# Attention scores: the products of two heads alternate between the upper and lower 64 rows of TensorE

## The chip, the cores and the metric

The kernel runs on one core of one Trainium2 chip. The metric is the device time of one execution in microseconds (us). Times of single runs are given as the median of three; the profile and the trace come from one further execution. TensorE is the matrix engine (PE in the rows, its weight loads PEld), VectorE is DVE, ScalarE is ACT, GpSimd is POOL, SyncE (SP) issues most DMAs.

## What is computed

Two decoder layers on 256 tokens of width 2048. Each layer has four mixers of width 512 side by side (a gated one, differential attention, dilated attention, a convolution), an output projection, and a feed-forward part of width 8192. The change touches the scores of the two attention mixers. Both come down to the same form for a pair of heads with 64 channels each:

```
s = q . k / sqrt(64)                       (per head, causal, 256 queries, 256 keys)
s = s - slope * distance,  masked where the distance is negative
p = softmax(s)                              (dilated: three patterns, summed by multiplicity)
```

Differential attention takes the difference of the two heads' probabilities; dilated attention keeps the two heads apart. Each mixer has four such pairs of heads, so there are eight pairs in a layer and 16 in all.

## The kernel before

**Large matmuls.** The weights (some 380 MB) come as 738 units of 128 x 1024 fp32. Each is split into a high part (ScalarE, tile `h`) and a low part (VectorE, tile `l`) in fp32r, a form of fp32 that TensorE takes in one pass, and three products of high and low parts are summed in PSUM (tiles `acc`, `acct`, `accu`, `accg`). The stages of a layer follow each other: the input projection with the mixers woven in, the output projection, then four blocks of the feed-forward part. A sublayer ends with a normalisation that the next projection must wait for (`sublayer_end`, tile `xhl`).

**The order of work.** It is written out by a planner in the program, before anything runs. Every engine is wrapped by `Paced`, which adds an estimated price per instruction (for a matmul: columns / 2400 us, four times that when the weights are plain fp32, plus 0.003). The mixers are generators: a `yield engine, time` means that the next instructions are written once TensorE's estimated clock has come that far. Between the large matmuls `pump()` runs whatever is due: splits of weights, evacuations, and steps of the mixers. On the chip each engine then takes its instructions in that order and waits on semaphores.

**The scores.** `scores` (lines 772 to 798) serves one pair of heads and is called by `dil_gen` and `diff_gen`, 16 times in all. `q` and `k` hold the two heads' channels in 128 partitions: head 0 in partitions 0 to 63, head 1 in 64 to 127, with tokens along the columns; they are plain fp32. The tile `ps` (tag `sc`) has 2 x 512 columns of PSUM, one bank per head, of which 384 are used: 128 for the first block of queries against the first block of keys, 256 for the second block of queries against both blocks. `COL` (line 770) names these two column ranges. For each head an identity matmul (`identb` times `ndist_sb`, bf16, all 128 rows) writes the negative distances into the 384 columns, and two products of 64 rows add `q . k` on top. Then VectorE takes the maximum over both heads (lines 785 and 787), ScalarE the exponential, and `give("sc")` frees the tile. `take("sc")` at its head makes the call wait until the tile is free.

The profile gives nearly all instructions the line of the wrapper, L99, so groups are told apart by the tiles' names: `sc<-ndist_sb,identb` is the identity matmul, `sc<-qk` a product of queries and keys.

Of the kernel before, what the change touches and what calls it, by code (L numbers as in the profile page):

```python
# [19 lines left out]
P = 128  # L20
L = 2
D = 2048
T = 256
# [111 lines left out]
def trunk_kernel(ctx, tc, xT, xt, wu, par, gpost, gw, gb, lam, ndist, mult, out):  # L135
# [16 lines left out]
    G, PE = nc.gpsimd, Paced(nc.tensor, _pe_cost)  # L152
# [147 lines left out]
    def take(name):  # L300
        while name in locks:
            yield None, lambda: name not in locks
        locks.add(name)
        yield PE, freed.get(name, 0.0) + D_

    def give(name):
        locks.discard(name)
        freed[name] = max(V.t, S.t)
# [103 lines left out]
    def unit_c(rhs):  # L412

        force(lambda: held[0] < 4)
        ps = pacc.tile([P, 2 * T], F32, tag="acc", name=f"acc{unit[0]}")
        for half in range(2):
            u = unit[0]
            unit[0] += 1

            for part in "hl":  # L420
                use(u, part == "l")
                for k in range(HALF):
                    if k % 2 == 0:
                        pump()
                    mm_c(ps, u, k, rhs, half * HALF + k, parts=part)
            done(u)
        return ps
# [342 lines left out]
    COL = (slice(0, P), slice(P, 3 * P))  # L770

    def scores(pr, q, k, s2, nm):

        yield PE, V.t + D_
        yield from take("sc")
        ps = psc.tile([P, 2, GW], F32, tag="sc", name="sc")
        for j in range(2):
            r = slice(64 * j, 64 * j + 64)
            PE.matmul(ps[:, j, 0 : 3 * P], identb, ndist_sb, start=True, stop=False)
            PE.matmul(ps[:, j, 0:P], q[r, 0:P], k[r, 0:P], start=False, stop=False)  # L780
            PE.matmul(ps[:, j, P : 3 * P], q[r, P:T], k[r, 0:T], start=False, stop=True)
        scored.append(1)
        yield V, PE.t + D_
        m = tiny.tile([P, 2, 2], F32, tag=nm + "m", name="m", bufs=1)
        V.reduce_max(m[:, :, 0], ps[:, :, 0:P], axis=AX.X)
        yield V, 0.0
        V.reduce_max(m[:, :, 1], ps[:, :, P : 3 * P], axis=AX.X)
        yield V, V.t
        V.tensor_tensor(m, m, nsl[:, pr], ALU.mult)
        yield S, V.t + D_  # L790
        l = tiny.tile([P, 2, 2], F32, tag=nm + "l", name="l", bufs=1)
        for j in range(2):
            for b in range(2):
                S.activation(s2[:, j, COL[b]], ps[:, j, COL[b]], AF.Exp, bias=m[:, j, b : b + 1], scale=SLOPE_PAIRS[pr][j], accum_out=l[:, j, b : b + 1])
            yield S, 0.0
        give("sc")
        yield V, S.t + D_
        return l
# [32 lines left out]
    def dil_gen(lane, li, pr, q, k, v, mhl, ready):  # L831
        nm = f"n{lane}"
        p = mx.tile([P, 2, 3 * P], F32, tag=nm + "s2", name="p2", bufs=1)
        yield from scores(4 + pr, q, k, p, nm)
        l = tiny.tile([P, 2, 2], F32, tag=nm + "l2", name="l2", bufs=1)
        for j in range(2):
            for b in range(2):
                V.scalar_tensor_tensor(p[:, j, COL[b]], p[:, j, COL[b]], 1.0, mult_sb[:, COL[b]], ALU.mult, ALU.mult, accum_out=l[:, j, b : b + 1])
                yield V, 0.0
        V.reciprocal(l, l)  # L840
        yield PE, V.t + D_
        pt = yield from transposed(p[:, 0], nm)
        yield from take("o")
        o = po.tile([P, 2, P], F32, tag="o", name="od")
        values(o, slice(0, 64), pt, v, slice(128 * pr, 128 * pr + 64))
        pt = yield from transposed(p[:, 1], nm)
        values(o, slice(64, 128), pt, v, slice(128 * pr + 64, 128 * pr + 128))
        yield S, PE.t + D_
        on = mx.tile([P, 2, P], F32, tag=nm + "on", name="on", bufs=1)
        for b in range(2):  # L850
            for j in range(2):
                S.activation(on[:, b, 64 * j : 64 * j + 64], o[:, b, 64 * j : 64 * j + 64], AF.Copy, scale=l[:, j, b : b + 1])
        give("o")
        yield from turned(on, mhl, pr, 1.0, ready)

    def diff_gen(lane, li, h, q, k, v, mhl, ready):
        nm = f"n{lane}"
        p = mx.tile([P, 2, 3 * P], F32, tag=nm + "s2", name="p2", bufs=1)
        l = yield from scores(h, q, k, p, nm)
        V.reciprocal(l, l)  # L860
        yield V, V.t
        V.tensor_scalar(l[:, 1], l[:, 1], lamv[:, li : li + 1], None, ALU.mult)
        yield S, V.t + D_
        for b in range(2):
            S.activation(p[:, 1, COL[b]], p[:, 1, COL[b]], AF.Copy, scale=l[:, 1, b : b + 1])
        for b in range(2):
            yield V, S.t + D_ if b == 0 else 0.0
            V.scalar_tensor_tensor(p[:, 0, COL[b]], p[:, 0, COL[b]], l[:, 0, b : b + 1], p[:, 1, COL[b]], ALU.mult, ALU.subtract)
        yield PE, V.t + D_
        pt = yield from transposed(p[:, 0], nm)  # L870
        yield from take("o")
        o = po.tile([P, 2, P], F32, tag="o", name="ob")
        values(o, slice(0, P), pt, v, slice(h * P, (h + 1) * P))
        yield S, PE.t + D_
        ss = tiny.tile([P, 2], F32, tag=nm + "oss", name="oss", bufs=1)
        on = mx.tile([P, 2, P], F32, tag=nm + "on", name="onb", bufs=1)
        for b in range(2):
            S.activation(on[:, b, :], o[:, b, :], AF.Square, accum_out=ss[:, b : b + 1])
        yield V, S.t + D_
        rs = yield from rsqrt(ss, P, [P, 2], nm + "ors")  # L880
        yield S, V.t + D_
        for b in range(2):
            S.activation(on[:, b, :], o[:, b, :], AF.Copy, scale=rs[:, b : b + 1])
        give("o")
        yield from turned(on, mhl, 4 + h, subg[:, li : li + 1], ready)
# [62 lines left out]
    for li in range(L):  # L948
# [72 lines left out]
        for n, (kind, grp, i) in enumerate(IN_ORDER[4:]):  # L1021
# [22 lines left out]
            ps = unit_c(xhl)  # L1044
# [31 lines left out]
        for blk in range(4):  # L1076
# [16 lines left out]
            j = 0  # L1093
# [9 lines left out]
            while j < KD:  # L1103
                ps = unit_c(xhl)
# [110 lines left out]
```

## Time and profile before

| | us |
|---|---|
| median of 3 runs | 2158.11 (2157.52 to 2159.85) |
| the profiled execution | 2158.0 |
| its span, first to last instruction | 2156.3 |
| TensorE busy | 2141.3 (99%) |
| VectorE busy | 1419.4 (66%) |
| ScalarE busy | 1093.9 (51%) |
| mean granted TensorE clock | 0.999 |

The span is what the trace shows; the time of an execution holds 1.7 us more. A matmul's duration in the trace runs from its start to the modelled arrival of its last result, so durations of neighbours overlap and a busy TensorE is not one that streams columns all the time; the distance from one start to the next says more. A weight load (PEld) may run beside a matmul.

### The profile page before, as it was taken

Reading aid. Unit: us, or ns where it says so; the run is one execution under the profiler, and the core shown is the slowest. Engines: PE = TensorE matmul, PEld = TensorE weight load, DVE = VectorE, ACT = ScalarE, POOL = GpSimd, SP = SyncE. Lnnn points to the kernel's source line nnn. Section 1 sums busy time; section 2 is a strip of 40 time slices with the busy share of each in tenths; the row PEclk is TensorE's granted clock in tenths of the full one; section 3 lists DMA queues with packets and bytes.
Section 4 is the critical chain, followed back from the end, with each engine's and each line's share of the span. In section 5 each row is a group of like instructions: output and inputs, shape, how many; then the busy total and the mean of one; then the engine's idle time right before and its main releaser. Section 6 shows DMA issues by size and latency. Waiting matters only on the chain.

```text
span 2156.3 us, 29992 instructions
## 1 busy us (share of the span) xinstructions
PE 2141.3 (99%) x11404; PEld 1830.0 (85%) x11404; DVE 1419.4 (66%) x2207; ACT 1093.9 (51%) x1709; POOL 10.5 (0%) x57
## 2 busy tenths in 40 slices
PE   9999999999999999999999999999999999999998
PEld 7888889888888888888888888898888888888887
DVE  6888756764665675575578886567646656746654
ACT  6656756554443453444465567465544434434542
POOL 0000000000000000000000000000000000000000
PEclk9999999999999999999999999999999999999999
DMA  7644564565555555555555445645655555555553
GB/s 240 234 141 163 179 214 146 194 226 194 194 186 188 194 188 190 193 190 185 168 169 164 157 152 190 207 149 193 224 195 190 186 192 195 186 188 193 188 188 112
DMA packets 110257, 400.21 MB, mean 186 GB/s; under 512 B 12512, under 2 KB 12800, under 8 KB 109344
## 3 DMA queue, kind: packets, MB, share of 16 engines
q1 hardware_dynamic: 109296, 393.93, 55.4%
q0 software_dynamic: 672, 4.36, 0.6%
q8 instruction: 89, 1.46, 0.3%
q14 instruction: 56, 0.46, 0.1%
q10 hardware_dynamic: 144, 0.01, 0.0%
HBM read 396.15 MB, written 2.10 MB: 185 GB/s over the span
## 4 chain that ended last, share of the span: by engine, by line
PE 97%; DVE 1%; DMA 1%; ACT 1%; issue 0%; DVEq 0%; ACTq 0%
PE acct L99 44%; PE acc L99 42%; PE accu L99 4%; PE accg L99 3%; PE sc L99 2%; DMA w<-in_wu 1%; PE od L99 0%; DVE X L99 0%; PE tr L99 0%; PE turned L99 0%; DVE xhl L99 0%; PE z L99 0%; ACT h L99 0%; DVE l L99 0%; PE ob L99 0%; DMA prm<-in_par 0%
## 5 line engine op out<-in xcount | busy, mean ns | idle before, releaser
L99 DVE TENSOR_TENSOR l<-w,h 128x1024 fp32r<-128x1024 f32 (+1 forms) x738 | 898.3, 1221 | 575.3 <-ACT h L99 571.9
L99 ACT ACTIVATE h<-w 128x1024 fp32r<-128x1024 f32 (+1 forms) x738 | 780.3, 1059 | 820.1 <-PE acct L99 445.4
L99 PE MATMUL acc<-xhl,h 128*128 128x512 f32 x2560 | 647.3, 394 | 0.0
L99 PE MATMUL acct<-h,f 128*128 128x512 f32 x1920 | 596.2, 391 | 0.0
L99 PEld LDWEIGHTS acc<-xhl,h 128*128 128x128 f32 x2560 | 459.2, 188 | 84.7 <-issue 2.0
L99 PEld LDWEIGHTS acct<-h,f 128*128 128x128 f32 x1920 | 360.5, 188 | 79.1
L99 PE MATMUL acct<-l,f 128*128 128x512 f32 x960 | 375.8, 391 | 0.0
L99 PEld LDWEIGHTS acc<-xhl,l 128*128 128x128 f32 x2560 | 348.2, 190 | 26.5 <-issue 1.3
L99 PE MATMUL acc<-xhl,l 128*128 128x256 f32 x2560 | 360.3, 283 | 0.0
L99 PEld LDWEIGHTS acct<-l,f 128*128 128x128 f32 x960 | 180.2, 188 | 38.7
L99 PE MATMUL acct<-h,xhl 128*128 128x512 f32 x512 | 168.1, 397 | 0.0
L99 PE MATMUL acct<-h,mhl 128*128 128x512 f32 x384 | 120.0, 391 | 0.0
L99 PEld LDWEIGHTS acct<-h,xhl 128*128 128x128 f32 x512 | 96.2, 188 | 19.6 <-issue 0.3
L99 DVE SCALAR_TENSOR_TENSOR cacc<-ch,prm,cacc 128x256 f32<-128x256 f32 x240 | 104.3, 486 | 0.0
L99 PE MATMUL acct<-l,xhl 128*128 128x512 f32 x256 | 99.9, 390 | 0.5 <-DVE l L99 0.5
L99 ACT ACTIVATE evr<-acc 128x256 f32<-128x256 f32 x160 | 61.4, 384 | 69.8 <-PE acc L99 69.3
L99 PE MATMUL accg<-xhl,h 128*128 128x256 f32 (+1 forms) x400 | 89.6, 325 | 5.4 <-DVE xhl L99 5.4
L99 PEld LDWEIGHTS acct<-h,mhl 128*128 128x128 f32 x384 | 72.1, 188 | 15.4
L99 PE MATMUL acct<-l,mhl 128*128 128x512 f32 x192 | 75.0, 390 | 0.0
L99 PEld LDWEIGHTS accg<-xhl,h 128*128 128x128 f32 x400 | 65.9, 193 | 10.7 <-DVE xhl L99 4.1
L99 DVE TENSOR_TENSOR u<-acc,evr 128x256 f32<-128x256 f32 x120 | 50.2, 419 | 11.0 <-ACT evr L99 10.9
L99 PEld LDWEIGHTS acct<-l,xhl 128*128 128x128 f32 x256 | 48.2, 188 | 9.7 <-DVE l L99 0.9
(182 smaller groups left out, 1379.8 us busy)
## 6 DMA issues: line engine op xcount, KB each, us to landing
w<-in_wu SPq DMA_DIRECT2D x734, 512.0 KB, 3.5
gpb<-in_gpost POOLq DMA_DIRECT2D x4, 1024.0 KB, 6.3
X<-in_xt SPq DMA_DIRECT2D x2, 1024.0 KB, 6.4
out<-X SPq DMA_DIRECT2D x8, 256.0 KB, 2.0
x_in<-in_xT SPq DMA_DIRECT2D x3, 512.0 KB, 6.0
w<-in_wu SPq DMA_DIRECT2D x4, 256.0 KB, 5.3
wT<-in_gw SPq DMA_DIRECT2D x2, 512.0 KB, 4.5
x_in<-in_xT SPq DMA_DIRECT2D x2, 256.0 KB, 4.5
```

Of the source, the lines that this page charges most:

```text
L99: return f(*a, **k)
```

## The change

The identity matmuls of both heads are issued first. Then the products follow block by block, and within a block head by head: head 0 first block, head 1 first block, head 0 second block, head 1 second block. Before, each head had its identity matmul and its two products in turn. The operands, the outputs, the number of matmuls and the flag of the last product of each head stay as they were.

```diff
         ps = psc.tile([P, 2, GW], F32, tag="sc", name="sc")
+
         for j in range(2):
-            r = slice(64 * j, 64 * j + 64)
             PE.matmul(ps[:, j, 0 : 3 * P], identb, ndist_sb, start=True, stop=False)
-            PE.matmul(ps[:, j, 0:P], q[r, 0:P], k[r, 0:P], start=False, stop=False)
-            PE.matmul(ps[:, j, P : 3 * P], q[r, P:T], k[r, 0:T], start=False, stop=True)
+        for b in range(2):
+            for j in range(2):
+                r = slice(64 * j, 64 * j + 64)
+                PE.matmul(ps[:, j, COL[b]], q[r, b * P : (b + 1) * P], k[r, 0 : (b + 1) * P], start=False, stop=b == 1)
         scored.append(1)
         yield V, PE.t + D_
```

## Rows read from the trace of the kernel before

**Rows 1.** The page: TensorE's and the other engines' busy time (share of the span, instructions), and the chain that ended last, by engine and by line.

```profile
PE 2141.3 (99%) x11404; PEld 1830.0 (85%) x11404; DVE 1419.4 (66%) x2207; ACT 1093.9 (51%) x1709; POOL 10.5 (0%) x57
...
PE 97%; DVE 1%; DMA 1%; ACT 1%; issue 0%; DVEq 0%; ACTq 0%
PE acct L99 44%; PE acc L99 42%; PE accu L99 4%; PE accg L99 3%; PE sc L99 2%; DMA w<-in_wu 1%; PE od L99 0%; DVE X L99 0%; PE tr L99 0%; PE turned L99 0%; DVE xhl L99 0%; PE z L99 0%; ACT h L99 0%; DVE l L99 0%; PE ob L99 0%; DMA prm<-in_par 0%
```

**Rows 2.** The busy time of each engine in the two stretches in which the scores lie. Columns: stretch, its length, busy us (instructions) of each engine, granted TensorE clock, DMA share, GB/s.

```profile
core 0: us, PE busy (x) PEld busy (x) DVE busy (x) ACT busy (x) POOL busy (x), PEclk, DMA share, GB/s
...
90.00:235.00 145.00, 145.00 (x801) 119.55 (x799) 124.77 (x274) 90.08 (x197) 1.60 (x1) 1.00 0.48 155
...
1160.00:1310.00 150.00, 150.00 (x832) 123.76 (x831) 125.84 (x279) 90.53 (x206) 1.55 (x1) 1.00 0.47 155
```

**Rows 3.** The waits of TensorE's matmuls: who waited for whom, us in total, times, the longest.

```profile
PE accg L99 <- DVE xhl L99: 5.4, 8, 1.9
PE warm L165 <- POOL epst L167: 1.1, 1, 1.1
PE acct L99 <- DVE l L99: 0.5, 1, 0.5
```

**Rows 4.** All instructions on the tile `sc`: weight loads and matmuls with count, duration in ns (min/median/max), first and last start, forms; and who waited for it (us, times).

```profile
L99 PEld LDWEIGHTS sc<-qk x128: 182/187/188, 93.2 to 1296.3; 64*128 64x128 f32 x128
L99 PE MATMUL sc<-qk x128: 272/374/378, 93.2 to 1296.5; 64*128 64x128 f32 x64, 64*128 64x256 f32 x64
...
L99 PE MATMUL sc<-ndist_sb,identb x32: 326/336/337, 92.9 to 1295.7; 128*128 128x384 bf16 x32
...
  DVE m L99: 24.9, 15
```

**Rows 5.** Timeline of TensorE's weight loads in the first call and up to the next unit. Columns: start us, us from the first to the last of the row, engine, line, operation, tile, form, count, and in brackets the idle time before it with what ended it.

```profile
92.93 0.10 PEld L99 LDWEIGHTS <-identb 128*128 128x128 bf16 x1
93.19 0.52 PEld L99 LDWEIGHTS sc<-qk 64*128 64x128 f32 x4 [0.17 <-DVE l L99]
94.04 0.10 PEld L99 LDWEIGHTS <-identb 128*128 128x128 bf16 x1 [0.33 <-issue]
94.31 0.52 PEld L99 LDWEIGHTS sc<-qk 64*128 64x128 f32 x4 [0.17 <-issue]
95.16 1.69 PEld L99 LDWEIGHTS acc<-xhl,h 128*128 128x128 f32 x8 [0.33 <-issue]
```

**Rows 6.** The same call in narrow windows, so that the first head's loads and matmuls stand apart (the first load row begins with the second load, the next with the third, and so on).

```profile
93.30 0.41 PEld L99 LDWEIGHTS sc<-qk 64*128 64x128 f32 x3
93.41 0.30 PEld L99 LDWEIGHTS sc<-qk 64*128 64x128 f32 x2
93.52 0.19 PEld L99 LDWEIGHTS sc<-qk 64*128 64x128 f32 x1
...
92.93 0.34 PE L99 MATMUL sc<-ndist_sb,identb 128*128 128x384 bf16 x1
93.20 0.37 PE L99 MATMUL sc<-qk 64*128 64x128 f32 x1
93.41 0.49 PE L99 MATMUL sc<-qk 64*128 64x128 f32 x2
93.52 0.59 PE L99 MATMUL sc<-qk 64*128 64x256 f32 x2
93.74 0.38 PE L99 MATMUL sc<-qk 64*128 64x256 f32 x1
```

**Rows 7.** The last of the 16 calls: weight loads, timeline.

```profile
1294.58 0.10 PEld L99 LDWEIGHTS <-identb 128*128 128x128 bf16 x1 [0.26 <-issue]
...
1296.82 0.20 PEld L99 LDWEIGHTS trd<-ident,onb 128*128 128x128 f32 x2 [0.33 <-issue]
```

**Rows 8.** The beginning of the fourth call: an fp32 transpose of 128 rows, then the identity in bf16, then the products of 64 rows; weight loads, then matmuls.

```profile
140.03 0.10 PEld L99 LDWEIGHTS <-identb 128*128 128x128 bf16 x1
140.39 0.52 PEld L99 LDWEIGHTS sc<-qk 64*128 64x128 f32 x4 [0.26 <-DVE cacc L99]
...
139.91 0.38 PE L99 MATMUL trd<-ident,on 128*128 128x128 f32 x2
140.13 0.33 PE L99 MATMUL sc<-ndist_sb,identb 128*128 128x384 bf16 x1
140.39 0.92 PE L99 MATMUL sc<-qk 64*128 64x128 f32 x4
```

**Rows 9.** Weight loads of fp32 products with 64 columns (probabilities times values), and of the unit behind them.

```profile
109.54 0.74 PEld L99 LDWEIGHTS od<-vt,pt 128*128 128x128 f32 x6 [0.33 <-issue]
110.21 0.54 PEld L99 LDWEIGHTS acc<-xhl,l 128*128 128x128 f32 x4
```

**Rows 10.** VectorE: the maximum of the first call on the timeline, and its longest wait in total (who waited for whom, us, times, the longest).

```profile
95.27 0.42 DVE L99 TENSOR_REDUCE m<-sc 128x2 f32<-128x256 f32 x1 [1.14 <-PE sc L99]
...
DVE l L99 <- ACT h L99: 571.9, 526, 3.0
```

## The prediction

> **What bounds the kernel now.** I read first the busy shares and the chain of waits of the page. TensorE is busy 99% of the span, and 97% of the chain that ended last runs through it; the score products ("sc") hold 2% of that chain [rows 1]. Second, the windows by stage. All sixteen calls of the changed function lie in two stretches, 90 to 235 us (layer 0) and 1160 to 1310 us (layer 1). There TensorE is busy 145.00 of 145.00 and 150.00 of 150.00 us, at a granted clock of 1.00 (2.4 GHz), while VectorE is busy 124.77 and 125.84 us, ScalarE about 90, and the DMA share is 0.48 [rows 2]. Third, the waits of TensorE: its matmuls wait 5.4 us for VectorE in the group that ends a sublayer, 0.5 us in a first unit, 1.1 us at the start, and for nothing in the scores [rows 3]. So time taken out of the scores on TensorE should come off the end, if the other engines follow.
>
> **What one call costs now.** The 16 calls make 32 identity matmuls (384 columns, bf16, 128 rows) and 128 product matmuls (64 rows, fp32): each fp32 product stands in the trace as two weight loads and two matmuls [rows 4]. The start of each instruction in the first call tells more than the durations, which overlap. Measured from the first identity load at 92.93, the first load of products stands at 93.19, the second identity at 94.04, its products at 94.31, and the next weights at 95.16 [rows 5]: 2.23 us a call, 1.12 us a head. The last call has 2.24 [rows 7], so the sixteen cost about 35.7 us, which is the 2% of the chain. One head, in steps [rows 5, 6]:
> - Identity, 92.93 to 93.19: 384 columns at 2.4 GHz are 0.16 us, and then 0.10 us follow in which nothing streams.
> - First product load, 93.19 to 93.30: 0.11 us, beside nothing.
> - Products 93.30 to 93.95. The starts lie 0.11 apart for 128 columns (93.41, 93.52) and 0.22 for 256 columns (93.52, 93.74), and the last of 0.21 ends at 93.95: 2 x 0.11 + 2 x 0.215, about 0.65 us. The other loads run beside them.
> - To the next identity load at 94.04: 0.09 us in which nothing streams.
>
> The two pauses of 0.09 and 0.10 are not waits for data: the load before the second head's products has the same 0.17 us idle before it as the first [rows 5]. Nor do they come from the change between bf16 and fp32: in the fourth call the identity's weights are loaded at 140.03 while a full-height fp32 transpose still streams, and its matmul starts 0.10 later, without a pause; the pause comes when the products' 64 rows follow, at 140.39 [rows 8]. I read them as the price of going between 128 rows and 64, and of the weights not being loaded ahead across it. [...]
>
> **What the change removes.** Both identity matmuls now come first, so the height changes twice a call and not four times. Gone are one change from products to identity (0.09) and one from identity to products (0.10 and the bare load of 0.11): 0.30 us a call. The second identity load (0.10 long [rows 5]) fits beside the first identity matmul of 0.16; without that cover it would cost at most 0.10. 16 x 0.30 = 4.8 us.
>
> **What it moves.** The four products of a call come as upper half (first block), lower half, upper, lower, and the two halves write different PSUM banks. Whether they stream beside each other, no row shows: in the trace of before an identity matmul always stands between the halves. The bounds for the eight product matmuls of a call:
> - Nothing overlaps, nothing is lost: 0.11 + 2 x 0.65 = 1.41 us.
> - The halves overlap and loads are free: a half still takes its own matmuls in order, and matmuls start in program order. Starts after the first load's end: 0, 0.11 (upper), 0.11, 0.22 (lower), 0.22, 0.43 (upper), 0.43, 0.65 (lower), end 0.86; with the load 0.97. Gain 0.44.
> - The halves overlap, and loads come one after another, 0.11 each. That is the rate in the rows: six loads of 64-column products take 109.54 to 110.21, 0.11 each, although such a product streams only half as long [rows 9]. The eight loads end at 0.11, 0.21, 0.32, 0.43, 0.54, 0.64, 0.75, 0.86. The products start at 0.11, 0.21, 0.32, 0.43, 0.54, 0.75 (its half is busy until then), 0.75 (the other half, its load just ended), 0.96, and end at 1.18. The gain is 1.41 - 1.18 = 0.23: one 256-column product hides behind another.
> - The lower bound below nothing: if each change of half is paid like a change of height, 0.09 + 0.11 = 0.20 for three changes, 0.60 lost.
>
> I take the third, gain 0.23: it keeps the load rate of the rows, and the operands, rows and banks of the two halves are apart. [...]
>
> **What else hangs on it.** No DMA is issued in the function and none is passed. The planner's clock adds the same six prices in another order (four per fp32 column, one per bf16 column), so it stands at the same time behind the call, and the order of all other instructions stays. The first products still wait for VectorE's q and k, now one identity (0.16) later, which only loosens that wait. The maximum on VectorE waits for the last product, the same one as before; VectorE sat idle 1.14 us for it in the first call and 24.9 us over all [rows 10, 4], so it starts earlier and nobody later. VectorE has 20 us free in the first stretch [rows 2], and 571.9 us of its waits are for ScalarE's high parts, which are paced by TensorE [rows 10]: a gain of 4 us a layer should pass through to the group that ends the sublayer.
>
> **Sum.** 0.30 + 0.23 = 0.53 us a call, 16 x 0.53 = 8.5 us. The profiled execution took 2158.0 us (2156.3 of span and 1.7 around it), 0.1 below the median of the runs, 2158.11. 2158.0 - 8.5 = 2149.5 us.
>
> **The rivals.**
> - No overlap: the products stay one after another, and only the two changes of height go. 2158.0 - 4.8 = 2153.2. For it: no row shows an overlap, and the two passes of one fp32 product always follow each other. Against it: nothing that the halves share is seen in the rows but the loads. This is also the case in which the alternation does nothing.
> - Full overlap, loads of one half beside loads of the other: 0.30 + 0.44 = 0.74, 16 x 0.74 = 11.8, 2146.2. For it: the loads read different partitions. Against it: 0.11 per load is the best rate in the rows. [...]
> - Slower: each change of half is a change to the array like a change of height. Then three changes come in (upper to lower, to upper, to lower) at 0.20 each, 0.60, against 0.30 removed: 0.30 x 16 = 4.8 us more, 2162.8. It decides from a price of 0.10 per change of half. For it: the rows show that a different set of rows costs 0.20, and none shows a change from rows 0 to 63 to rows 64 to 127 without it. Against it: those changes were all of height.
> - The gain is taken up: VectorE, at 86% of the first stretch, comes late with the low parts of the weights and TensorE waits for it. Then 2158, as before. For it: that share; against it: TensorE shows no such wait in the scores [rows 3].
>
> **How the numbers follow.** Chances: overlap with loads in a row 36%, full overlap 16%, no overlap 28%, change of half paid 12%, gain taken up 8%. 0.2% of 2158 is 4.3 us, about what a measurement of this kernel can tell from no change. The first two are faster by more than that; no overlap (4.8) lies close to the bound and is so in 6 of 10, with the other 4 in the same; the paid change (4.8) splits 7 to 5 between slower and same, and the gain taken up is mostly the same. That gives 0.69 faster, 0.22 same, 0.09 slower. The range goes from 2145 (full overlap and 1 us of spread) to 2157 (no overlap with most of its gain lost on the way), and leaves out the last two cases, 2 in 10.
>
> **What would show it.** In the timeline of a call: two identity matmuls 0.16 apart; half of the 32 idle stretches of 0.33 before an identity load gone; the next unit's weights 1.69 us behind the first identity load (1.93 without overlap, 1.49 with full overlap, 2.53 if each change of half is paid). In the waits: no new TensorE wait in 90 to 235 us. The start of the lower half's 256-column product tells directly: together with the upper half's second one, or 0.2 behind it. The prediction is wrong if a call doesn't shorten to between 1.5 and 1.95 us, or if it does and TensorE then waits for VectorE.

## The result and the profile after

The changed kernel takes 2142.82 us (median of four runs, 2142.68 to 2144.22) against 2157.89 for the kernel before beside it: a ratio of 0.9929, 95% interval 0.9915 to 0.9943. That is 15.1 us less. The forecast was 8.5 us less, 2149.5, with a range from 2145 to 2157: right in sign, wrong in size, outside the range. The profiled execution went from 2158.0 to 2142.68 us, its span from 2156.3 to 2140.9.

From the page: busy times, and the chain by line. These answer to [rows 1]:

```profile
PE 2126.4 (99%) x11404; PEld 1821.1 (85%) x11404; DVE 1419.6 (66%) x2207; ACT 1092.3 (51%) x1709; POOL 11.1 (1%) x57
...
PE acct L99 45%; PE acc L99 42%; PE accu L99 4%; PE accg L99 3%; PE sc L99 1%; DMA w<-in_wu 1%; PE od L99 0%; DVE X L99 0%; PE tr L99 0%; PE turned L99 0%; PE z L99 0%; PE ob L99 0%; DVE xhl L99 0%; DVE ssx L99 0%; DMA prm<-in_par 0%
```

TensorE makes the same 11404 matmuls and is 14.9 us less busy, the scores fall from 2% of the chain to 1%, and the other engines' busy times hardly move. The gain is all TensorE's. The timeline of the first call, weight loads and then matmuls, answers to [rows 5]:

```profile
92.78 0.11 PEld L99 LDWEIGHTS <-identb 128*128 128x128 bf16 x2
93.21 0.52 PEld L99 LDWEIGHTS sc<-qk 64*128 64x128 f32 x8 [0.32 <-DVE l L99]
94.06 0.30 PEld L99 LDWEIGHTS acc<-xhl,h 128*128 128x128 f32 x2 [0.33 <-issue]
...
92.78 0.50 PE L99 MATMUL sc<-ndist_sb,identb 128*128 128x384 bf16 x2
93.21 0.93 PE L99 MATMUL sc<-qk 64*128 64x128 f32 x8
```

The call takes 94.06 - 92.78 = 1.28 us from its first identity load to the next unit's weights, where it took 2.23. The other fifteen calls save the same 0.95. Sixteen times 0.95 are 15.2 us, the whole change of the time to within 0.2. The two identity matmuls start 0.17 us apart (92.78 and 92.95), where the prediction counted 0.16 for 384 columns at 2.4 GHz; by estimate from durations in the trace of before, 391 ns for 512 columns (`acct<-h,f`) and 283 for 256 (`accu<-h,f`) at a granted clock of 1.00, a column takes 0.42 ns, some 2.4 a ns. The eight product loads now take 0.52 us in all, as long as four did before. Narrow windows of the same call show why (loads, then matmuls):

```profile
93.21 0.18 PEld L99 LDWEIGHTS sc<-qk 64*128 64x128 f32 x1 [0.32 <-DVE l L99]
93.21 0.19 PEld L99 LDWEIGHTS sc<-qk 64*128 64x128 f32 x2 [0.32 <-DVE l L99]
93.32 0.30 PEld L99 LDWEIGHTS sc<-qk 64*128 64x128 f32 x4
...
93.53 0.59 PE L99 MATMUL sc<-qk 64*128 64x256 f32 x3
93.53 0.60 PE L99 MATMUL sc<-qk 64*128 64x256 f32 x4
```

The first row stops at 93.211 us, the second 9 ns later, and the second holds one load more, whose end comes 0.01 us after the first's: the two loads began within 0.01 us of each other, one in each half. They go on in pairs (four from 93.32), and all four 256-column matmuls lie in 0.60 us, which two of them took before [rows 6]. In this call both halves ran the whole of their products side by side: eight matmuls took 0.93 us where four of one half took 0.92 [rows 8]. TensorE waits for nobody new:

```profile
90.00:235.00 145.00, 145.00 (x836) 121.33 (x835) 130.24 (x284) 95.96 (x208) 1.75 (x1) 1.00 0.52 168
...
PE accg L99 <- DVE xhl L99: 5.2, 8, 1.6
PE acct L99 <- DVE l L99: 0.2, 1, 0.2
```

The first row is the first stretch of [rows 2]. It holds 836 matmuls where it held 801, VectorE is busy 130 of 145 us, and TensorE still has no gap. The other two, with the same 1.1 us at the start, are all the waits of TensorE's matmuls; none is longer than in [rows 3].

### The profile page after: what moved, and what is told of

It is laid out like the page before. It is cut to its first block, busy times and chain, and to the rows that moved or that the text cites. A ratio compares the mean times of both kernels' runs of the same rounds, so it can differ in the third digit from the quotient of the medians.

```text
span 2140.9 us, 29992 instructions
## 1 busy us (share of the span) xinstructions
PE 2126.4 (99%) x11404; PEld 1821.1 (85%) x11404; DVE 1419.6 (66%) x2207; ACT 1092.3 (51%) x1709; POOL 11.1 (1%) x57
## 4 chain that ended last, share of the span: by engine, by line
PE 97%; DVE 1%; DMA 1%; ACT 0%; issue 0%; DVEq 0%; ACTq 0%
PE acct L99 45%; PE acc L99 42%; PE accu L99 4%; PE accg L99 3%; PE sc L99 1%; DMA w<-in_wu 1%; PE od L99 0%; DVE X L99 0%; PE tr L99 0%; PE turned L99 0%; PE z L99 0%; PE ob L99 0%; DVE xhl L99 0%; DVE ssx L99 0%; DMA prm<-in_par 0%
## 5 line engine op out<-in xcount | busy, mean ns | idle before, releaser
L99 PEld LDWEIGHTS acct<-h,mhl 128*128 128x128 f32 x384 | 72.1, 188 | 15.3
```

Of the source, the lines that this page charges most:

```text
L99: return f(*a, **k)
```

## The experiments

Calls are given from the first identity load to the next unit's weights unless said otherwise. Edits are shown against the changed kernel, that of "Identities apart" against the kernel before; in code, `...` stands for lines left out.

**Heads in turn.** The grouping of the identities without the alternation:

```diff
-        for b in range(2):
-            for j in range(2):
-                r = slice(64 * j, 64 * j + 64)
+        for j in range(2):
+            r = slice(64 * j, 64 * j + 64)
+            for b in range(2):
                 PE.matmul(ps[:, j, COL[b]], q[r, b * P : (b + 1) * P], k[r, 0 : (b + 1) * P], start=False, stop=b == 1)
```

> The identities come first, then head 0's two products, then head 1's two: the grouping without the alternation. From the first identity load to the next unit's weights a call took 2.235 us before and 1.286 us in the changed kernel. Theory A (each half of the array works through its own loads and products and does not wait for the other): the halves still run side by side, 1.29 us, 2142.8 us in all, and the first product of the lower half starts with the first of the upper. Rival B (a product starts only after every earlier product has begun its first pass): the lower half begins 0.21 later, 1.50 us, 2146.2. Rival C (loads and matmuls strictly in program order, the two passes of a product one behind the other): it begins 0.43 later, 1.72 us, 2149.7. Rival D (the overlap needs neighbours of the two halves): nothing overlaps, 1.93 us, 2153.1.

Measured: 2143.05 us, ratio 0.9932 (0.9917 to 0.9947), as fast as the changed kernel. Weight loads of its first call:

```profile
93.66 0.11 PEld L99 LDWEIGHTS <-identb 128*128 128x128 bf16 x2
94.09 0.53 PEld L99 LDWEIGHTS sc<-qk 64*128 64x128 f32 x8 [0.32 <-DVE l L99]
94.95 0.30 PEld L99 LDWEIGHTS acc<-xhl,h 128*128 128x128 f32 x2 [0.33 <-issue]
```

1.29 us a call; the eight loads take 0.53, in pairs again. Theory A held at this distance (a later run finds its limit), B, C and D fell. Head 1's products did not wait for head 0's ahead of them in the program: the second load began 13 ns behind the first, where loads of one half lie 0.11 us apart [rows 6]. The alternation itself gave 0.01 us a call; what stood between the heads before was the second identity matmul of 128 rows.

**One half.** The changed order, all products in the upper half; head 1 then takes head 0's channels:

```diff
-                r = slice(64 * j, 64 * j + 64)
+                r = slice(0, 64)
```

> The changed order, but both heads' products take the channels of partitions 0 to 63: head 1's own queries and keys are left out, and all products use the upper half. If the overlap hangs on the halves being different: products and loads one behind the other, 2 x 0.65 us of products, 1.93 us a call, 2153.1 us in all, which is what the two saved changes of height give alone. If the order alone made the gain (rival): 1.29 us and 2142.8.

Measured: 2153.39 us, ratio 0.998 (0.997 to 0.9989). Weight loads of the first call:

```profile
93.02 0.11 PEld L99 LDWEIGHTS <-identb 128*128 128x128 bf16 x2
93.45 1.17 PEld L99 LDWEIGHTS sc<-qk 64*128 64x128 f32 x8 [0.32 <-issue]
94.96 0.19 PEld L99 LDWEIGHTS acc<-xhl,h 128*128 128x128 f32 x1 [0.33 <-issue]
```

The loads take 1.17 us in place of 0.52, and the call 1.94 (with the starts in nanoseconds 1.935, where the kernel before has 2.235 and the changed one 1.286). So the overlap came only with products of both halves; that the two heads write different PSUM banks, as they do here too, did not bring it. The two saved changes of height alone give 2.235 - 1.935 = 0.30 us a call. The overlap gives the rest, 1.935 - 1.286 = 0.65.

**Identities cut by block.** Two changes of height come back while the products overlap:

```diff
-        for j in range(2):
-            PE.matmul(ps[:, j, 0 : 3 * P], identb, ndist_sb, start=True, stop=False)
         for b in range(2):
             for j in range(2):
+                PE.matmul(ps[:, j, COL[b]], identb, ndist_sb[:, COL[b]], start=True, stop=False)
+            for j in range(2):
...
+                PE.matmul(ps[:, j, COL[b]], q[r, b * P : (b + 1) * P], k[r, 0 : (b + 1) * P], start=False, stop=True)
```

> The identity is cut in two: 128 columns for both heads, the first block's products, then 256 columns for both heads, the second block's products. The columns and the alternation stay; two changes of height come back. If a change to 128 rows costs 0.09 and one to 64 rows 0.10 and a bare fp32 load of 0.11, as the rows of before gave: 1.286 + 0.30 = 1.59 us a call, 2142.8 + 4.8 = 2147.6. Rival (those pauses came from the order of before, not from the height): 1.29 us and 2142.8.

Measured: 2148.0 us, ratio 0.9956 (0.9941 to 0.9971).

```profile
94.40 0.11 PEld L99 LDWEIGHTS <-identb 128*128 128x128 bf16 x2
94.62 0.30 PEld L99 LDWEIGHTS sc<-qk 64*128 64x128 f32 x4
95.04 0.11 PEld L99 LDWEIGHTS <-identb 128*128 128x128 bf16 x2
95.37 0.30 PEld L99 LDWEIGHTS sc<-qk 64*128 64x128 f32 x4 [0.21 <-issue]
96.00 0.19 PEld L99 LDWEIGHTS acc<-xhl,h 128*128 128x128 f32 x1 [0.33 <-ACT h L99]
```

1.60 us a call, 0.31 more than the changed kernel for the same columns and the same overlap: a pair of changes of height cost 0.30 us where it was taken out and 0.31 where it was put in. In both runs the height changes together with the data type (identity in bf16, products in fp32); what tells the two apart comes with the identities last, below.

**Identities apart.** All four changes of height, with the second block's products of head 0 moved behind head 1's first:

```diff
+        for b, j, ident_ in ((0, 0, True), (0, 1, True), (1, 0, False), (1, 1, False)):
...
+            if ident_:
+                PE.matmul(ps[:, j, 0 : 3 * P], identb, ndist_sb, start=True, stop=False)
...
```

> Identity 0, head 0 first block, identity 1, head 1 first block, head 0 second block, head 1 second block: all four changes of height as before, the alternation only behind the second identity. With overlap of the halves the last three products take the lower half's 0.65 us, head 0's second product lies beside: 2.235 - 0.43 = 1.80 us a call, 2151.1 us. Without overlap 2.24 us and 2158.

Measured: 2151.32 us, ratio 0.9971 (0.9959 to 0.9982). Weight loads of the first call:

```profile
93.21 0.10 PEld L99 LDWEIGHTS <-identb 128*128 128x128 bf16 x1
93.48 0.29 PEld L99 LDWEIGHTS sc<-qk 64*128 64x128 f32 x2 [0.17 <-DVE l L99]
93.90 0.10 PEld L99 LDWEIGHTS <-identb 128*128 128x128 bf16 x1
94.17 0.52 PEld L99 LDWEIGHTS sc<-qk 64*128 64x128 f32 x6 [0.17 <-issue]
95.02 0.19 PEld L99 LDWEIGHTS acc<-xhl,h 128*128 128x128 f32 x1 [0.33 <-ACT h L99]
```

The call takes 1.81 us, as the first case says: behind the second identity six loads fit into the 0.52 us of four. Only the products with no identity between them overlapped here.

**More of the upper half ahead.** Since the heads in turn had overlapped, the next runs put more of the upper half in front of the lower: products cut into pieces of 32 and of 16 columns.

```diff
...
+                for c in range(0, (b + 1) * P, 32):
+                    PE.matmul(ps[:, j, b * P + c : b * P + c + 32], q[r, b * P : (b + 1) * P], k[r, c : c + 32], start=False, stop=b == 1 and c + 32 == 2 * P)
```

> As the run with the heads in turn, but each head's products are cut into pieces of 32 columns: 12 products, so 24 loads and 24 matmuls of the upper half stand in the program before the first of the lower half. A half is then bound by its loads, 24 x 0.107 = 2.57 us. If the halves stay independent that far ahead: 0.43 + 2.57 + 0.12 = 3.12 us a call, 2172 us. If the lower half comes only when the upper is nearly done: up to 5.7 us a call, 2213 us; where loads begin to come in pairs on the timeline tells how far ahead TensorE looks.

> The same with pieces of 16 columns: 48 loads and 48 matmuls of the upper half ahead of the lower. Independent halves: 0.43 + 48 x 0.107 + 0.11 = 5.68 us a call, 2213 us. A limited look-ahead: the loads run singly at first and in pairs from some point, up to 10.8 us a call and 2295 us.

Measured: one run each, 2253.43 and 2413.96 us, both above the upper end that was expected, so these sizes missed. For the first of the two, weight loads around the start of the lower half in the first call, and stretches of the tile's work with the granted clock after the engines' busy times (PE, PEld, DVE, ACT); the last two rows are of the third call of the run with 16 columns:

```profile
96.83 0.33 PEld L99 LDWEIGHTS sc<-qk 64*128 64x128 f32 x3
97.17 0.33 PEld L99 LDWEIGHTS sc<-qk 64*128 64x128 f32 x4
...
94.72:96.94 2.22, 2.22 (x21) 2.22 (x20) 0.00 (x0) 0.00 (x0) 1.00 0.64 220
96.98:97.30 0.32, 0.32 (x8) 0.32 (x8) 0.00 (x0) 0.00 (x0) 1.00 0.52 128
98.00:101.00 3.00, 3.00 (x16) 3.00 (x16) 0.00 (x0) 0.00 (x0) 0.50 0.36 131
...
157.76:162.68 4.92, 4.92 (x45) 4.92 (x45) 0.00 (x0) 0.00 (x0) 1.00 0.35 110
162.70:163.00 0.30, 0.30 (x8) 0.30 (x8) 0.00 (x0) 0.00 (x0) 1.00 0.00 0
```

From 94.72 to 96.94 the loads come singly, 20 in 2.22 us, 0.11 apart. Then they come doubly, 8 touching a stretch of 0.32, and after the upper half has finished singly again. The first load of the lower half is the 22nd: three matmuls of the upper half's 24 had not begun. The halves thus overlapped only at the seam. With 16 columns, in a call that was still at a granted clock of 1.00 up to there, it is the 46th: again three, of 48.

The excess over the expected upper ends, 40 and 119 us, goes with a lower clock: in the lower half's lone stretch of the first run the granted clock is 0.50 and the loads lie some 0.2 us apart, 16 touching 3.00 us; before it fell, TensorE had run nothing but 64-row products of 32 columns since the call's identities. The mean granted clock is 0.978 and 0.947 where the changed kernel has 0.999, by estimate a loss of some 47 us of 2252 and 125 us of 2412.

**Six matmuls a half, at a granted clock of 0.999.** Pieces of 128 columns, three per head, first heads in turn (below), then alternating, with the two loops exchanged:

```diff
+        for j in range(2):
+            for n in range(3):
...
+                PE.matmul(ps[:, j, n * P : (n + 1) * P], q[r, (n > 0) * P : ((n > 0) + 1) * P], k[r, (n == 2) * P : ((n == 2) + 1) * P], start=False, stop=n == 2)
```

> Heads in turn again, but the second block's product is cut into two of 128 columns, so 6 loads and 6 matmuls of the upper half stand ahead of the lower half's first. The columns are the same. In the run with 4 and 4 ahead the lower half's first load began 13 ns behind the upper's, with 3 loads and 3 matmuls of the upper half still to come; in the run with 24 and 24 ahead it began when again about 3 and 3 were left. If TensorE looks some six instructions ahead: the lower half begins when the upper's third matmul starts, 0.2 to 0.3 us behind, 1.5 to 1.6 us a call, 2146 to 2148 us. Rival (it looks far ahead, and the run with small pieces was held up by something else): 1.29 us and 2142.8. Rival (halves overlap only when nothing of the other half waits): 1.93 us and 2153.

> The same six products of 128 columns, alternating between the halves. Nothing of the other half stands more than one product ahead: 1.29 us a call and 2142.8 us, by every theory in which neighbours of different halves overlap. If the cutting itself costs (more loads), it shows here: each further pass pair at most 0.02 us, 1.33 us and 2143.5.

Measured: 2148.06 us in turn (ratio 0.9954, 0.9937 to 0.997) and 2143.26 alternating (0.9933, 0.9918 to 0.9948). Weight loads of the first call in turn, and below the dots two narrow windows of it; then the first call of the alternating run:

```profile
93.55 0.12 PEld L99 LDWEIGHTS <-identb 128*128 128x128 bf16 x2
93.98 1.07 PEld L99 LDWEIGHTS sc<-qk 64*128 64x128 f32 x12 [0.32 <-DVE l L99]
95.17 0.30 PEld L99 LDWEIGHTS acc<-xhl,h 128*128 128x128 f32 x2
...
94.20 0.19 PEld L99 LDWEIGHTS sc<-qk 64*128 64x128 f32 x1
94.31 0.19 PEld L99 LDWEIGHTS sc<-qk 64*128 64x128 f32 x2
```

```profile
92.91 0.11 PEld L99 LDWEIGHTS <-identb 128*128 128x128 bf16 x2
93.34 0.75 PEld L99 LDWEIGHTS sc<-qk 64*128 64x128 f32 x12 [0.32 <-DVE l L99]
94.21 0.30 PEld L99 LDWEIGHTS acc<-xhl,h 128*128 128x128 f32 x2
```

In turn, the loads run alone at 93.98, 94.09 and 94.20, and the first pair begins at 94.31, 0.33 behind: again with three of the upper half's six matmuls left, counting the one that begins in the pair. The twelve loads take 1.07 us in turn and 0.75 alternating, the call 1.62 against 1.30. Here the alternation was worth 4.8 us, while with the kernel's own four matmuls per head it was worth 0.01 us a call: there exactly three stand in front of the lower half once the first has begun.

**Identities last.** A version that the price of a change of height points to:

```diff
-        for j in range(2):
-            PE.matmul(ps[:, j, 0 : 3 * P], identb, ndist_sb, start=True, stop=False)
...
+                PE.matmul(ps[:, j, COL[b]], q[r, b * P : (b + 1) * P], k[r, 0 : (b + 1) * P], start=b == 0, stop=False)
+        for j in range(2):
+            PE.matmul(ps[:, j, 0 : 3 * P], identb, ndist_sb, start=False, stop=True)
```

> The identities are issued last: the alternating products open the accumulation, the two identity matmuls close it. The height still changes twice a call. Theory (a pause of 0.09 to 0.10 at each change of height, and the first fp32 load behind it beside nothing): the call begins with the pause 0.09 and the bare load 0.11 of the products, but the bare load before the identity is the short bf16 one, and the next unit's fp32 load is no longer bare, since the identity has its height: 0.11 us less a call, 1.7 us in all, 2141.1. Rival (nothing is won, since the products now wait for q and k where the identity covered it, or the next unit's load stays bare): 2142.8 or more.

It ran beside the changed kernel on the same chip:

> The changed kernel once more, to stand beside the next run on the same chip: 2142.8 us, 1.286 us a call.

Measured: 2140.67 us (2140.47 to 2141.3; ratio 0.9919, 0.9905 to 0.9932) against 2142.89 for the changed kernel (2142.61 to 2144.6; 0.993, 0.9917 to 0.9944). The two intervals against the kernel before overlap, but no run of the one reaches a run of the other, and the 2.2 us agree with the 1.7 expected. Weight loads of its first call, and below the dots the seventh call's loads with the matmuls in front of them:

```profile
92.66 0.52 PEld L99 LDWEIGHTS sc<-qk 64*128 64x128 f32 x8
93.52 0.11 PEld L99 LDWEIGHTS <-identb 128*128 128x128 bf16 x2 [0.33 <-issue]
93.70 0.82 PEld L99 LDWEIGHTS acc<-xhl,h 128*128 128x128 f32 x4
...
200.22 0.83 PE L99 MATMUL ob<-vt,pt 128*128 128x128 f32 x6
200.98 0.52 PEld L99 LDWEIGHTS sc<-qk 64*128 64x128 f32 x8
```

The next unit's weights have no idle stretch of 0.33 before them any more; they are loaded at 93.70, beside the identity matmuls, which last from 93.52 to 94.02 in the trace. This is the fastest version here.

This run also tells height from data type. From the bf16 identity to the unit's weights at 93.70 in the first call the type changes and the height stays, and no idle stretch is marked. At the head of the seventh call both sides are plain fp32 and the height changes: six matmuls of 128 rows and 128 columns begin at 200.22, by their 0.83 us some 0.11 apart, and have by estimate streamed by 200.89; the first load of 64 rows stands at 200.98, the same 0.09 behind. The kernel before shows the way back, from 64 rows to 128:

```profile
108.69 0.52 PEld L99 LDWEIGHTS sc<-qk 64*128 64x128 f32 x4 [0.17 <-issue]
```

The next loads are those of the plain fp32 products of 128 rows at 109.54, with the usual 0.33 idle before them, and the unit behind those, of the same height, has none [rows 9].

## Why the prediction was wrong in size

- **TensorE bounds the scores, and what it saves comes off the end:** right. 15.2 us saved in the calls, 15.3 in the profiled time; VectorE at 90% of the first stretch did not hold it up, so that rival fell.
- **Two changes of height fewer, 0.30 us a call:** right. 0.30 by the one-half run, 0.31 by the run that puts them back. Those two runs change height and data type together; the run with the identities last tells them apart: 0.09 where the height alone changes (200.98), no idle stretch where the type alone does (93.70).
- **The products' overlap, "I take the third, gain 0.23":** the step that failed. It measured 0.65. The call took 1.28 where the text gave 1.70. Two assumptions were wrong, each for want of a row. "Loads come one after another, 0.11 each" was read from loads of 128 rows and of one half; in the changed kernel loads of different halves began within 0.01 us of each other. And "matmuls start in program order", with the two passes of a product back to back, set the stated upper bound at 0.44; in the changed kernel's trace the lower half's first product starts within 0.01 us of the upper half's first, and with the heads in turn its first load begins 13 ns behind, with three matmuls of the upper half still to begin, so the bound should have been one head's whole stream, 0.65. With it the sum is (0.30 + 0.65) x 16 = 15.2 and the time 2142.8. The range was too narrow for the same reason: its lower end was that false bound. By the prediction's own sign it was wrong: a call outside 1.5 to 1.95 us.
- **Full overlap as a rival, 2146.2:** its picture of the loads was the right one (eight in 0.52 us), its price came from the same program order.
- **Slower by paid changes of half:** fell. In the run that alternates pieces of 128 columns the half changes five times a call in program order, 1.00 us at the rival's 0.20 each, and the twelve loads take 0.75 us in all.
- **No overlap, 2153.2:** fell for this kernel. Its number was right for the run with one half, 2153.39.
- **The alternation as the cause:** the text weighed the new order of the products; the run in turn shows that moving the identity out from between the heads was enough.
- **The 32 idle stretches of 0.33 before an identity load:** misread. Only the second identity of a call has 0.33; the first has none or 0.26 [rows 5, 7]. It changes no term of the sum.

## What to carry to other kernels

Where products contract over 64 rows, put the work of the upper and of the lower half next to each other, with no matmul of 128 rows in between: here eight loads of both halves then took the 0.52 us of four, and the call 0.65 us less than with all products in one half. The halves wrote different PSUM banks; one bank for both was not tried. Alternate them when a half brings more matmuls than the four of this kernel: six in turn cost 4.8 us here, four 0.01 us a call; five were not tried. Change the height as seldom as the work allows: a pair of changes cost 0.30 to 0.31 us here, two pauses of 0.09 and 0.10 and a load of 0.11 beside nothing. Let the first load behind a change be a short one: with the bf16 identity there in place of a unit's fp32 weights, the kernel was 2.2 us faster, 0.14 a call, where the estimate was the bare load's 0.11. Where two streams may be independent, let the range reach to the longer of the two alone.

## What the runs showed that was not expected

- Loads of the two halves ran at the same time: eight took 0.52 us in the changed kernel, where eight of one half took 1.17.
- TensorE began the lower half's work while about three matmuls of the upper half, ahead of it in the program, had not begun. That was so with 4 matmuls in front (13 ns behind the upper half's first load), with 6 (0.33 us behind, in a pair with the upper half's fourth), with 24 (the 22nd load) and with 48 (the 46th). What sets the number was not tried.
- While products of 32 columns ran, with loads 0.11 us apart, the granted clock fell from 1.00 to 0.50 inside a single call, though TensorE showed no idle time (busy 3.00 of 3.00 us at 0.50).
